# A list scheduler's figures at the second norm of a decoder layer: longer planned times, two loads counted as landed, the scaled epsilon on its own

## The chip, the cores and the metric

The kernel runs on one core of a Trainium2 chip. The metric is the device time of one execution in microseconds (us), lower is better. TensorE (PE in the profile) multiplies, VectorE (DVE) and ScalarE (ACT) do elementwise work, SyncE (SP) and GpSimd (POOL) issue most of the transfers.

## The reference

One layer of a hybrid decoder trunk on 256 tokens and 16 learned meta tokens, width 2048, all in fp32. Two token mixers and their gates give `h`, and the part that matters here follows:

```python
h = h + rms_norm(m @ w_o[l], g_post_mix[l])
u = rms_norm(h, g_pre_mlp[l])                       # the second norm
f = jnp.square(jax.nn.relu(u @ w_up[l])) @ w_down[l]   # 2048 -> 8192 -> 2048
h = h + rms_norm(f, g_post_mlp[l])                  # the third norm
```

## The kernel before

Every fp32 weight is loaded in chunks of 1 MB and split in two fp32r parts that TensorE can multiply: ScalarE casts the high part (`hi`), VectorE subtracts it from the raw chunk (`lo`). The MLP runs in pieces of 1024 hidden columns. A product of the up projection (U...) uses a chunk of 1024 rows by 256 columns, 128 of the columns for each of two banks. Names of products: `U1a0` is an up product of half 1, pair a, first half of the rows of w_up; `U1a1` the second half; both write the banks u0 and u1, as `U1b0` and `U1b1` do after them. `X...` are down products into the banks x00 to x11, `P...` and `Q...` are products of a Strassen-like scheme.

Around the second norm the order is: the last up products of pair 0 (`last_of_first`, into x00 to x11, called acc_up in the profile), then `FIRST_PIECE = "U1a0 U1a1 U1b0 R U1b1"` (L1388), then X3. The up products start on `h` that is not normed yet: the norm's factor of each token is applied later. For this, eight squares (`square_h1`, ScalarE, one for each token tile and block of 512 columns; L987 in the profile) add up the rows, `mean2` (VectorE, L1540 and L1541) and `root2` (ScalarE, L1545) give the root, and `diag2` (VectorE) makes the factor `r2` with a Newton step (L446 to L450), splits it in a power of two `p2` (L1550) and a mantissa, writes `p2` into a diagonal (L1553) and works out a scaled epsilon `eps2` from the mantissa (L1554 to L1558). The power of two goes through TensorE (`R`: `rows2`, L478) to `rb` (L1846); relu times `rb` (L1603) follows, and `u2` itself is multiplied by it (`scale_u2`, L1566). The mantissa is left out of the up and down products and comes back only as `eps2` in the third norm, at the end of the kernel (`norm3.start` in `before_last`).

After each pair of up products `up_pair` adds the two halves of the bank: ScalarE copies the one (L1578), VectorE adds the other (L1585). The next product into the same bank waits for that.

The order of the instructions on each engine in this part comes from a list scheduler that runs while the kernel is built (`Plan`, L23). Each item has an engine, a planned cost, and names that it reads and writes; `late` is added to the time until its result is there (a transfer's landing), and 0.15 (`HOP`) when the result goes to another engine. TensorE and SyncE keep the order in which their items were added. A due time is worked backwards: TensorE's items are due when the planned costs of the products ahead of them are used up, and all others so early that the items after them can be on time:

```python
due[i] = min(due[i], due[a] - cost - late - self.HOP)
...
first = min(begin(i) for i in can)
i = min((i for i in can if begin(i) <= first + self.HOP), key=lambda i: (due[i], i))
```

So on each engine, of the items that could begin within 0.15 of the earliest, the one due first is taken; an item with a late due time still takes a gap if nothing else can begin. The instructions are written out in the order of the planned starts, and each engine then works strictly in that order and waits by semaphores. The planned costs say nothing to the chip but this order.

The chunks of this part are loaded into five rooms (`raw_a`, `raw_c`, and three called `raw_m`) by `load` (L1449), in the order in which they are used: raw_a for U1b0, raw_c for U1b1, then X3 and so on; a room is loaded again when its chunk has been split (`split_raw`, L1487: cast on ScalarE at L1496, low part on VectorE at L1500). `kept` (L1830) stores `h` to memory for the end. The `bring` items (L1518) are loads by GpSimd's queue that add onto a chunk in its room.

Of the kernel before, what the change touches and what calls it, by code (L numbers as in the profile page):

```python
# [10 lines left out]
I32 = mybir.dt.int32  # L11
AF = mybir.ActivationFunctionType
ALU = mybir.AluOpType
# [102 lines left out]
def hybrid_block(ctx: ExitStack, tc: tile.TileContext, ins: dict, out: bass.AP):  # L116
    nc = tc.nc
# [34 lines left out]
    def f32(ap):  # L152
        return ap.bitcast(F32)
# [12 lines left out]
    late = []  # L166
# [34 lines left out]
    NB = D // CW  # L201
# [174 lines left out]
    ssq = const.tile([P, NT + 1, 2], F32, name="ssq")  # L376
# [67 lines left out]
    def rsqrt(r, q, var):  # L444

        nc.vector.reciprocal(r, q)  # L446
        nc.vector.tensor_mul(q, r, r)
        nc.vector.tensor_mul(q, q, var)
        nc.vector.tensor_scalar(q, q, -0.5, 1.5, op0=ALU.mult, op1=ALU.add)
        nc.vector.tensor_mul(r, r, q)  # L450
# [359 lines left out]
    def block(n):  # L810
        return slice(n * CW, (n + 1) * CW)
# [131 lines left out]
    h1 = big.tile([P, NT, D], F32, tag="k8", bufs=2, name="h1")  # L943
# [41 lines left out]
    def square_of(src, norm, t, n, scale=1.0):  # L985
        junk = tmp.tile([P, CW], F32, tag="junk", bufs=1, name=f"sq_{norm}_{n}_{t}")
        nc.scalar.activation(junk, src, AF.Square, scale=scale, accum_out=norm[:, t, n:n + 1])  # L987
# [14 lines left out]
    plan = Plan()  # L1002
# [20 lines left out]
    room_at = {(1, 0): 0, (2, 0): 1}  # L1023
# [176 lines left out]
    for i, s in enumerate(steps):  # L1200
# [5 lines left out]
        if s == "X30":  # L1206
            for t in range(NT):
                plan.add("PE", 0.0, lambda t=t: banks_o.update({f"c{t}3": acc_tile(f"o_c{t}3")}),
                         writes=(f"c{t}3", f"c{t}0"))
# [8 lines left out]
        if s == "X13":  # L1218
            for t in range(NT):
                plan.add("DVE", 0.4, lambda t=t: norm1.start(t), reads=(f"ssq{t}",),  # L1220
                         writes=(f"v{t}",))
# [142 lines left out]
    for b in range(2):  # L1364
        room = big.tile([P, b * LINE + KD * T], F32R, tag=f"s{b}", name=f"forms_{b}")
# [21 lines left out]
    plan = Plan()  # L1387
# [27 lines left out]
    def source(what, i):  # L1415
        if what[0] == "U":
            h, pr, c = int(what[1]), "ab".index(what[2]), int(what[3])
            return columns(w_up, c * HALF[0], HALF[0], i * PF + h * CW + pr * HALF_CW, HALF)[0]
        h, n = AT[what]
        return columns(w_down, (i * 2 + h) * KH, KH, n * CW)[0]  # L1420
# [26 lines left out]
    room_at = {}  # L1447

    def load(r):  # L1449
        src, (rows, width) = source(*r)  # L1450
        room = room_at[r] = free_rooms.pop(0)
        plan.add("SP", 3.1, lambda: nc.sync.dma_start(
            room_of[room].rearrange("p (k c) -> p k c", k=rows), src),
            writes=(f"raw{room}",), late=3.6)

    def loads():
        while to_load and free_rooms:
# [72 lines left out]
    ssq2 = const.tile([P, NT, NB], F32, name="ssq2")  # L1530
    r2, p2, eps2 = (const.tile([P, NT], F32, name=n) for n in ("r2", "p2", "eps2"))
    EXPONENT, MANTISSA, ONE = 0x7F800000, 0x007FFFFF, 0x3F800000
    box2 = {}

    def square_h1(t, n):
        return lambda: square_of(h1[:, t, block(n)], ssq2, t, n)
# [9 lines left out]

    def diag2():
        rsqrt(r2, box2["q"], box2["v"])
        bits, p_bits, e_bits = (x_.bitcast(I32) for x_ in (r2, p2, eps2))
        nc.vector.tensor_scalar(p_bits, bits, EXPONENT, None, op0=ALU.bitwise_and)  # L1550
        box2["diag"] = tmp.tile([P, T], F32R, tag="junk", bufs=1, name="diag2")
        for t in range(NT):
            nc.vector.tensor_scalar_mul(box2["diag"][:, t * P:(t + 1) * P], ident, p2[:, t:t + 1])  # L1553
        nc.vector.tensor_scalar(e_bits, bits, MANTISSA, ONE, op0=ALU.bitwise_and,  # L1554
                                op1=ALU.bitwise_or)
        for _ in range(2):
            nc.vector.tensor_mul(eps2, eps2, eps2)
        nc.vector.reciprocal(eps2, eps2)  # L1558
        nc.vector.tensor_scalar(eps2, eps2, RMS_EPS, None, op0=ALU.mult)
# [4 lines left out]
    def scale_u2(g):  # L1564
        both_ = u2[:, g * CK:(g + 1) * CK].rearrange("p k a t -> p (k a) t")
        plan.add("DVE", 2.22, lambda: nc.vector.tensor_mul(  # L1566
            both_, f32(both_), rb[:, None, :T].broadcast_to([P, 2 * CK, T])),
            reads=("rb",), writes=(f"u2{g // 2}",))
# [71 lines left out]
    def free_from(h, i):  # L1640

        return max(last_reader.get((h_, i), -1) for h_ in range(h + 1))

    def into_forms(h, pr, i, s_name, box):
        G, A, ks = forms[h], f"A{h}{pr}", slice(2 * pr, 2 * pr + 2)

        n = 2 if h or i == NP - 1 or "X1" in MODES[i] else 1

        def dst(part):
            return G[:, A1:A1 + n, ks, part, :]  # L1650

        def src():
            return box["s"].rearrange("p j (f t) -> p f j t", f=2)[:, :n]
        if i < NP - 1 and h == 1:
            def a_(f):
                return box["s"][:, :, f * P:(f + 1) * P]
            plan.add("DVE", 0.35, lambda: nc.vector.scalar_tensor_tensor(
                Q[:, S2Q, ks, :], Q[:, S3Q, ks, :], -1.0, a_(A2), op0=ALU.mult, op1=ALU.subtract),
                reads=(s_name, f"q3{pr}"), writes=(f"q3{pr}",))
            plan.add("DVE", 0.35, lambda: nc.vector.tensor_add(  # L1660
                Q[:, S4Q, ks, :], a_(A1), Q[:, S2Q, ks, :]),
                reads=(s_name, f"q3{pr}"), writes=(f"q4{pr}",))
        plan.add("ACT", 0.1 + 0.215 * n, lambda: nc.scalar.copy(dst(0), src()), reads=(s_name,),
                 writes=(A,))
        plan.add("DVE", 0.08 + 0.27 * n, lambda: nc.vector.tensor_sub(dst(1), src(), f32(dst(0))),
                 reads=(s_name, A), writes=(A + "l",))
        if i == NP - 1:
            return
        if h == 0 and pr == 1:
            split_form(0, S3, "S3", S3Q, "q3")  # L1670
        if h == 1 and pr == 1:
            split_form(0, S1, "S1", S1Q, "q1")
            split_form(1, S2, "S2", S2Q, "q3")
            split_form(1, S4, "S4", S4Q, "q4")
# [148 lines left out]
    for j in range(4):  # L1823
        plan.add("PE", 1.36, last_of_first(j), reads=(f"hi{q0}", f"lo{q0}"),
                 writes=(f"x{j // 2}{j % 2}",))
    loads()
    for t in range(NT):
        for n in range(NB):
            plan.add("ACT", 0.65, square_h1(t, n), reads=("h1",), writes=("junk", "ssq2"))
    kept = dram.tile([P, NT, D], F32, name="kept_h1")  # L1830
    plan.add("SP", 6.4, lambda: nc.sync.dma_start(kept, h1), writes=("h1", "hi3", "lo3"), late=4.0)
    plan.add("DVE", 0.4, mean2, reads=("ssq2",), writes=("v2",))
    plan.add("ACT", 0.3, root2, reads=("v2",), writes=("q2",))
    plan.add("DVE", 1.2, diag2, reads=("q2", "v2"), writes=("diag2",))
    for pr in range(2):
        up_done(0, pr, 0, accs[2 * pr:2 * pr + 2], [f"x{pr}{j}" for j in range(2)])

# [2 lines left out]
    for at_step[0], (s, i) in enumerate(steps):  # L1840
        for rest in [rest for rest in deferred if at_step[0] > free_from(rest[0], rest[2] - 1)]:
            deferred.remove(rest)
            into_forms(*rest)
        if s == "R":
            plan.add("PE", 0.9, rows2, reads=("diag2",), writes=("b",))
            plan.add("DVE", 0.4, lambda: nc.vector.tensor_copy(rb[:, :T], banks["b"][:, :T]),  # L1846
                     reads=("b",), writes=("rb",))
            for rest in unscaled:
                relu_squared(*rest)
            continue  # L1850
        if s[:3] == "add":
            continue
        for w in range(m_, min(m_ + 4, len(products))):
            if before.get(w, -1) >= m_:
                break
            weights(w)
        if m_ >= tail:
            break
        {"U": product_up, "X": product_plain, "P": product_block, "Y": product_last,
         "Q": product_block}[s[0]](m_, s, i)  # L1860
        m_ += 1
        if (s, i) == ("U1b1", 0):
            for g in range(KD // CK):
                scale_u2(g)

# [4 lines left out]
             writes=(f"raw{room_g}",), late=2.0)  # L1872
    for t in range(NT):
        plan.add("SP", 3.1, lambda t=t: nc.sync.dma_start(room_of[rooms_h[t]][:, :D], kept[:, t]),
                 reads=("h1",), writes=(f"raw{rooms_h[t]}",), late=2.0)
# [10 lines left out]
    def sum_of_squares(t, n):  # L1886
        src, name = tokens_of(t, n)
        plan.add("ACT", 0.65, lambda: square_of(src, norm3.ssq, t, n), reads=(name,),
                 writes=("junk", f"ssq{t}{n}"))

    def times_g(t, n):
        src, name = tokens_of(t, n)
        plan.add("DVE", 0.62, lambda: nc.vector.tensor_mul(
            dst_of(t, n * CW, (n + 1) * CW), src, g_mlp[:, block(n)]),
            reads=(name, f"raw{room_g}"), writes=(f"out{t}{n}", name if n < 2 else f"raw{room_f}"))

    def before_last(t):

        sum_of_squares(t, NB - 2)
        times_g(t, NB - 2)  # L1900
        plan.add("DVE", 0.4, lambda: norm3.start(t, eps2[:, t:t + 1]),
                 reads=[f"ssq{t}{n}" for n in range(NB - 1)], writes=(f"v{t}",))

    for t in range(NT):
        for n in range(NB - 2):
# [37 lines left out]
    for e, cs in enumerate(col_halves):  # L1943
        for w, s in ends:
# [3 lines left out]
                reads=half_names(w) + act_names(h, A2), writes=("ab"[e],))  # L1948

        def half_done(e=e, cs=cs):  # L1950
# [6 lines left out]
            if e == 0:  # L1957
# [12 lines left out]
                 writes=("junk", "v1", f"raw{room_f}", "out13") + (("r1",) if e else ()))  # L1970
# [28 lines left out]
```

## Time and profile before

| what | value |
|---|---|
| timed runs | median 1194.74 us (1194.17, 1194.74, 1195.89) |
| profiled execution, its own time | 1199.05 us |
| its span, first to last instruction | 1197.3 us |
| mean granted TensorE clock | 0.996 |
| PE, DVE, ACT busy | 1180.4, 1020.5, 680.9 us |
| all waits of TensorE that the view of waits lists | 8.5 us |

The table is read from the top down: the timed runs are what counts, the profiled execution is where durations come from. It took 1.75 us more than its span, and 4.31 us more than the timed median. In the rows of the timeline the columns are start, duration, engine, line, operation, result<-operands, shapes and count, and in square brackets the idle time of the engine ahead of the row and what ended it. Rows with a count above 1 are merged.

### The profile page before, as it was taken

What the parts mean: (1) busy time and instruction counts of PE and PEld (TensorE: products, weight loads), DVE (VectorE), ACT (ScalarE), POOL (GpSimd) and SP (SyncE); (2) the same over time, 40 slices, a digit from 0 to 9 for tenths busy, and PEclk for the clock granted to TensorE, in tenths of its full rate; (3) what the DMA queues carried; (4) which work ended last, traced back from release to release, by engine and by line L of the source; (5) the groups of instructions that cost most, each with busy time, mean ns of one, the idle gap of its engine ahead of it and who ended that gap; (6) DMA issues with size and microseconds to landing.
All of it is one profiled execution on the core that took longest, in us unless ns stands there. A gap on an engine that the chain in (4) does not pass through costs nothing.

```text
span 1197.3 us, 15759 instructions
## 1 busy us (share of the span) xinstructions
PE 1180.4 (99%) x6363; PEld 1023.7 (85%) x6363; DVE 1020.5 (85%) x1097; ACT 680.9 (57%) x705; POOL 41.8 (3%) x48
## 2 busy tenths in 40 slices
PE   9999999999999999999999999999999999999997
PEld 9999988888888888897888888888888888887886
DVE  6899978999776778677988989899999889898965
ACT  6533344444583455565666657666666676676742
POOL 1000000000000000000000000000000000000000
PEclk9999999999999999999999999999999999999999
DMA  9655555656548578548779889898998988998971
GB/s 291 212 177 179 185 197 179 207 179 205 182 165 282 172 251 264 198 135 290 211 210 260 242 243 273 248 262 230 274 249 253 259 265 243 250 262 232 271 255 71
DMA packets 176811, 269.76 MB, mean 225 GB/s; under 512 B 4610, under 2 KB 92866, under 8 KB 175841
## 3 DMA queue, kind: packets, MB, share of 16 engines
q1 hardware_dynamic: 160432, 234.83, 59.1%
q0 software_dynamic: 15408, 32.66, 14.9%
q10 hardware_dynamic: 896, 1.25, 0.3%
q8 instruction: 50, 0.82, 0.3%
q14 instruction: 25, 0.20, 0.0%
HBM read 264.53 MB, written 4.19 MB: 224 GB/s over the span
## 4 chain that ended last, share of the span: by engine, by line
PE 87%; DMA 6%; DVE 2%; ACT 2%; issue 2%; DVEq 0%; POOLq 0%; ACTq 0%; SPq 0%
PE acc_gate L789 15%; PE bank_u L496 14%; PE bank_a L1715 9%; PE bank_u L502 7%; PE acc_up L1715 7%; PE o_c L1128 6%; DMA raw_m<-in_w_down_dram 6%; PE bank_b L1715 5%; PE acc_z L491 4%; PE acc_co L789 4%; PE acc_po L789 4%; PE acc_v L491 3%; PE acc_g L491 3%; PE acc_vg L491 2%; PE bank_u L1715 1%
## 5 line engine op out<-in xcount | busy, mean ns | idle before, releaser
L496 PE MATMUL bank_u<-m,hi 128*128 128x512 f32 x960 | 331.1, 391 | 2.6 <-DVE F_raw L1585 2.6
L502 PE MATMUL bank_u<-m,lo 128*128 128x256 f32 x960 | 265.9, 277 | 0.0
L276 ACT CAST hi<-raw 128x2048 fp32r<-128x2048 f32 (+2 forms) x94 | 151.0, 1619 | 191.5 <-PE acc_gate L789 64.0
L1500 DVE TENSOR_TENSOR lo<-raw_m,hi 128x2048 fp32r<-128x2048 f32 x85 | 194.4, 2287 | 34.2 <-ACT hi L1496 34.2
L496 PEld LDWEIGHTS bank_u<-m,hi 128*128 128x128 f32 x960 | 180.9, 188 | 41.1 <-DVE F_raw L1585 3.0
L279 DVE TENSOR_TENSOR lo<-raw,hi 128x2048 fp32r<-128x2048 f32 (+2 forms) x94 | 180.1, 1924 | 37.1 <-ACT hi L276 36.4
L1496 ACT CAST hi<-raw_m 128x2048 fp32r<-128x2048 f32 x85 | 161.8, 1911 | 75.1 <-PE bank_a L1715 23.0
L502 PEld LDWEIGHTS bank_u<-m,lo 128*128 128x128 f32 x960 | 180.9, 188 | 1.6
L789 PE MATMUL acc_gate<-hi,u_um 128*128 128x512 f32 x416 | 131.1, 389 | 0.0
L557 DVE SCALAR_TENSOR_TENSOR c<-a,taps,c 128x256 f32<-128x256 f32 x240 | 115.6, 483 | 6.8
L789 PEld LDWEIGHTS acc_gate<-hi,u_um 128*128 128x128 f32 x416 | 78.1, 188 | 16.1
L789 PE MATMUL acc_gate<-lo,u_um 128*128 128x512 f32 x208 | 80.9, 389 | 0.0
L1715 PE MATMUL bank_a<-hi,forms 128*128 128x512 f32 (+1 forms) x232 | 75.7, 388 | 4.1 <-DVE F_raw L1744 4.1
L1715 PE MATMUL bank_b<-hi,forms 128*128 128x512 f32 (+1 forms) x208 | 67.4, 386 | 0.0
L1128 PE MATMUL o_c<-hi,m 128*128 128x512 f32 x208 | 65.6, 390 | 0.0
L1578 ACT COPY half<-bank_u 128x256 f32<-128x256 f32 x60 | 22.3, 372 | 73.6 <-PE bank_u L502 73.6
L1715 PE MATMUL bank_a<-fourth_pair,forms 128*128 128x512 f32 (+1 forms) x252 | 59.9, 386 | 0.7 <-ACT st_Q L1753 0.7
L1500 DVE TENSOR_TENSOR lo<-raw_a,hi 128x2048 fp32r<-128x2048 f32 x21 | 48.0, 2286 | 12.4 <-ACT hi L1496 12.4
L1715 PEld LDWEIGHTS bank_a<-hi,forms 128*128 128x128 f32 x232 | 43.4, 188 | 15.1 <-issue 5.2
L1500 DVE TENSOR_TENSOR lo<-raw_c,hi 128x2048 fp32r<-128x2048 f32 x20 | 45.7, 2287 | 10.9 <-ACT hi L1496 10.9
L1715 PEld LDWEIGHTS bank_a<-fourth_pair,forms 128*128 128x128 f32 x252 | 45.2, 188 | 10.1 <-ACT st_Q L1753 1.1
L1496 ACT CAST hi<-raw_a 128x2048 fp32r<-128x2048 f32 x21 | 40.1, 1910 | 20.6 <-PE bank_u L496 10.8
(398 smaller groups left out, 2267.2 us busy)
## 6 DMA issues: line engine op xcount, KB each, us to landing
raw<-in_w_in_dram SPq DMA_DIRECT2D x52, 1024.0 KB, 5.1
raw_m<-in_w_up_dram SPq DMA_DIRECT2D x42, 1024.0 KB, 7.2
raw_m<-in_w_down_dram SPq DMA_DIRECT2D x35, 1024.0 KB, 5.3
raw_a<-in_w_down_dram SPq DMA_DIRECT2D x15, 1024.0 KB, 5.7
raw_c<-in_w_down_dram SPq DMA_DIRECT2D x14, 1024.0 KB, 5.8
raw_m<-in_w_down_dram POOLq DMA_DIRECT2D x12, 1024.0 KB, 10.8
raw_o<-in_w_o_dram SPq DMA_DIRECT2D x10, 1024.0 KB, 7.2
raw_a<-in_w_up_dram SPq DMA_DIRECT2D x9, 1024.0 KB, 7.5
```

Of the source, the lines that this page charges most:

```text
L276: nc.scalar.copy(hi[:, sl, cs], raw[:, sl, cs])
L279: nc.vector.tensor_sub(lo[:, sl, cs], raw[:, sl, cs], f32(hi[:, sl, cs]))
L491: nc.tensor.matmul(acc, w[:, k[0], cs], act[:, k[1], a, off:], start=first and n == 0, stop=last and n == 2)
L496: nc.tensor.matmul(acc.rearrange("p (a t) -> p a t", a=2)[:, :, ts], hi[:, k[0], cs], act[:, k[1], :, off + ts.start:off + ts.stop], start ...
L502: nc.tensor.matmul(acc[:, :T], lo[:, k[0], cs], act[:, k[1], 0, off:], start=False, stop=stop, skip_group_check=True)
L557: nc.vector.scalar_tensor_tensor(c, conv["a"][:, q, i:i + T], taps[:, q, i:i + 1], c, op0=ALU.mult, op1=ALU.add)
L789: nc.tensor.matmul(acc, act(kk)[:, a_, ts_], w_[:, k, :], start=kk == 0 and n == 0, stop=kk == nk - 1 and n == 2)
L1128: nc.tensor.matmul(acc, form(k, a_), box[w_][:, k, :], start=start and k == 0 and n == 0, stop=stop and k == CK - 1 and n == 2, skip_group ...
L1496: nc.scalar.copy(box["hi"], raw)
L1500: nc.vector.tensor_sub(box["lo"], raw, f32(box["hi"]))
L1578: nc.scalar.copy(box[j], accs[j][:, :T])
L1715: nc.tensor.matmul(acc, forms[h][:, f, k, a_, :], box[w_][:, k, cs], start=start and k == 0 and n == 0, stop=stop and k == KH - 1 and n == ...
```

## The change

The first two loads of the last plan are planned with no cost on SyncE's queue and a landing after 1 and 2 instead of 3.1 and 3.6. The squares are planned at 0.75 instead of 0.65, `diag2` at 1.7 instead of 1.2. The five instructions of the scaled epsilon leave `diag2` and become an item of VectorE of their own (`eps_of_scaled`), planned at 0.9; it is added to the list behind U1b1 of the second piece, and `norm3.start` now names `eps2` as what it reads, so that its due time comes from there.

```diff
@@ -1449,9 +1449,10 @@
     def load(r):
         src, (rows, width) = source(*r)
         room = room_at[r] = free_rooms.pop(0)
-        plan.add("SP", 3.1, lambda: nc.sync.dma_start(
+        ahead = len(room_at) <= 2
+        plan.add("SP", 0.0 if ahead else 3.1, lambda: nc.sync.dma_start(
             room_of[room].rearrange("p (k c) -> p k c", k=rows), src),
-            writes=(f"raw{room}",), late=3.6)
+            writes=(f"raw{room}",), late=len(room_at) if ahead else 3.6)
@@ -1546,13 +1547,15 @@
     def diag2():
         rsqrt(r2, box2["q"], box2["v"])
-        bits, p_bits, e_bits = (x_.bitcast(I32) for x_ in (r2, p2, eps2))
+        bits, p_bits = (x_.bitcast(I32) for x_ in (r2, p2))
         nc.vector.tensor_scalar(p_bits, bits, EXPONENT, None, op0=ALU.bitwise_and)
         box2["diag"] = tmp.tile([P, T], F32R, tag="junk", bufs=1, name="diag2")
         for t in range(NT):
             nc.vector.tensor_scalar_mul(box2["diag"][:, t * P:(t + 1) * P], ident, p2[:, t:t + 1])
-        nc.vector.tensor_scalar(e_bits, bits, MANTISSA, ONE, op0=ALU.bitwise_and,
-                                op1=ALU.bitwise_or)
+
+    def eps_of_scaled():
+        nc.vector.tensor_scalar(eps2.bitcast(I32), r2.bitcast(I32), MANTISSA, ONE,
+                                op0=ALU.bitwise_and, op1=ALU.bitwise_or)
         for _ in range(2):
             nc.vector.tensor_mul(eps2, eps2, eps2)
         nc.vector.reciprocal(eps2, eps2)
@@ -1826,12 +1829,12 @@
-            plan.add("ACT", 0.65, square_h1(t, n), reads=("h1",), writes=("junk", "ssq2"))
+            plan.add("ACT", 0.75, square_h1(t, n), reads=("h1",), writes=("junk", "ssq2"))
...
-    plan.add("DVE", 1.2, diag2, reads=("q2", "v2"), writes=("diag2",))
+    plan.add("DVE", 1.7, diag2, reads=("q2", "v2"), writes=("diag2",))
@@ -1862,6 +1865,8 @@
             for g in range(KD // CK):
                 scale_u2(g)
+        if (s, i) == ("U1b1", 1):
+            plan.add("DVE", 0.9, eps_of_scaled, reads=("diag2",), writes=("eps2",))
@@ -1899,7 +1904,7 @@
         plan.add("DVE", 0.4, lambda: norm3.start(t, eps2[:, t:t + 1]),
-                 reads=[f"ssq{t}{n}" for n in range(NB - 1)], writes=(f"v{t}",))
+                 reads=["eps2"] + [f"ssq{t}{n}" for n in range(NB - 1)], writes=(f"v{t}",))
```

## The prediction

> **What bounds the kernel now.** I read the page first, for who is busy; then the waits of TensorE; then the stretch around its longest wait, engine by engine in order of time. Page of the profile:
>
> ```profile
> span 1197.3 us, 15759 instructions
> ## 1 busy us (share of the span) xinstructions
> PE 1180.4 (99%) x6363; PEld 1023.7 (85%) x6363; DVE 1020.5 (85%) x1097; ACT 680.9 (57%) x705; POOL 41.8 (3%) x48
> ```
>
> TensorE is busy for 1180.4 of 1197.3 us. A scheduler that leaves the products alone can win only what TensorE waits, and what it runs slowly because it waited. Two lines of the view of waits, TensorE's own (total, times, longest):
>
> ```profile
> PE bank_a L1715 <- DVE F_raw L1744: 4.1, 3, 1.7
> PE bank_u L496 <- DVE F_raw L1585: 2.6, 1, 2.6
> ```
>
> The second line is the longest single wait, and it is in the stage that the diff touches: U1b0 cannot write bank u0 before VectorE has added up the two halves of U1a (L1585). Windows around it, and one behind another wait, for the granted clock (PEclk):
>
> ```profile
> core 0: us, PE busy (x) PEld busy (x) DVE busy (x) ACT busy (x) POOL busy (x), PEclk, DMA share, GB/s
> 542.00:547.60 5.60, 5.60 (x34) 4.70 (x32) 4.38 (x15) 3.11 (x4) 0.00 (x0) 1.00 1.11 415
> 547.60:550.25 2.65, 0.00 (x2) 0.00 (x1) 2.65 (x4) 2.17 (x2) 0.00 (x0) 0.97 0.94 362
> 550.25:553.56 3.31, 3.31 (x10) 2.83 (x11) 2.47 (x2) 0.00 (x0) 0.00 (x0) 0.51 1.04 352
> 553.56:557.45 3.89, 3.89 (x25) 3.38 (x24) 0.00 (x0) 0.00 (x0) 0.00 (x0) 1.00 1.06 375
> 1089.24:1092.55 3.31, 3.31 (x15) 2.75 (x16) 3.31 (x2) 3.28 (x3) 0.00 (x0) 1.00 0.60 187
> ```
>
> TensorE does nothing for 2.65 us, and then runs at a granted clock of 0.51 for 3.31 us: ten matmuls, which at the rate of the first row (5.60 / 34 = 0.165 us) take 1.65. So the wait costs 2.65 + 1.66 = 4.3 us. Why was VectorE late? Its timeline:
>
> ```profile
> 540.81 0.16 DVE L1540 TENSOR_REDUCE tot<-ssq 128x2 f32<-128x8 f32 x1 [0.95 <-ACT ng_offset=None)_3_1_4612 L987]
> 541.01 0.17 DVE L1541 TENSOR_SCALAR tot<-tot 128x2 f32<-128x2 f32 x1
> 541.08 0.41 DVE L1585 TENSOR_TENSOR F_raw<-half,acc_up 128x256 f32<-128x256 f32 x1
> 542.88 2.29 DVE L1500 TENSOR_TENSOR lo<-raw_a,hi 128x2048 fp32r<-128x2048 f32 x1 [1.38 <-ACT hi L1496]
> 545.08 0.16 DVE L446 RECIPROCAL r<-rs_q 128x2 f32<-128x2 f32 x1
> ...
> 546.67 0.16 DVE L1554 TENSOR_SCALAR eps<-r 128x2 int32<-128x2 int32 x1
> ...
> 547.57 2.29 DVE L1500 TENSOR_TENSOR lo<-raw_c,hi 128x2048 fp32r<-128x2048 f32 x1
> 549.78 0.74 DVE L1585 TENSOR_TENSOR F_raw<-half,bank_u 128x256 f32<-128x256 f32 x2
> 550.44 2.28 DVE L1500 TENSOR_TENSOR lo<-raw_m,hi 128x2048 fp32r<-128x2048 f32 x1
> 557.76 0.42 DVE L1846 COPY rb<-bank_b 128x256 f32<-128x256 f32 x1 [5.04 <-PE bank_b L478]
> ...
> 561.69 1.28 DVE L1665 TENSOR_TENSOR forms<-F_raw,forms 128x512 fp32r<-128x512 f32 x2
> ```
>
> Ahead of the sums of U1a (549.78) stand, without a pause, the low part of raw_a, diag2 (545.08 to 546.67), the scaled epsilon (546.67 to 547.57) and the low part of raw_c. The first of them waited for ScalarE's cast of raw_a. ScalarE's timeline:
>
> ```profile
> 532.59 1.91 ACT L276 CAST hi<-raw 128x2048 fp32r<-128x2048 f32 x1 [2.39 <-DMA raw<-in_w_up_dram]
> 534.40 0.62 ACT L987 ACTIVATE ng_offset=None)_0_0_4564<-h 128x512 f32<-128x512 f32 x1
> ...
> 540.06 0.63 ACT L987 ACTIVATE ng_offset=None)_3_1_4612<-h 128x512 f32<-128x512 f32 x1
> 540.59 0.19 ACT L987 ACTIVATION_READ_ACCUMULATOR ng_offset=None)_3_1_4612<-h 128x1 f32 x1
> 540.69 0.35 ACT L1578 COPY half<-acc_up 128x256 f32<-128x256 f32 x1
> 540.94 1.91 ACT L1496 CAST hi<-raw_a 128x2048 fp32r<-128x2048 f32 x1
> 542.74 0.20 ACT L1545 ACTIVATE rs_q<-tot 128x2 f32<-128x2 f32 x1
> 542.84 1.90 ACT L1496 CAST hi<-raw_c 128x2048 fp32r<-128x2048 f32 x1
> 544.92 0.37 ACT L1578 COPY half<-bank_u 128x256 f32<-128x256 f32 x1 [0.18 <-PE bank_u L502]
> 547.64 0.37 ACT L1578 COPY half<-bank_u 128x256 f32<-128x256 f32 x1 [2.35 <-PE bank_u L502]
> ```
>
> All eight squares and four half copies come ahead of the cast of raw_a, and they start at 534.40, because the cast before them waited for a load.
>
> **The change part by part.** No multiplication, transfer or byte is added; the cost of the diff is an order. I work the order out by hand from the scheduler's rules (costs and due times are the ones in the code; they say who goes first, and I take no time from them). Zero is the first product of last_of_first; TensorE's planned costs put U1a0 at 5.44 (4 x 1.36), U1a1 at 10.88, U1b0 at 16.32 and R at 21.76 (2 x 2.72 each).
>
> Loads. Planned before, raw_a landed at 3.1 + 3.6 + 0.15 = 6.85, behind all squares (8 x 0.65 + 4 x 0.28 = 6.32). Now it has landed at 1.15, and its cast can begin as soon as last_of_first has let go of its buffer: 5.44 + 0.15 = 5.59. Its low part is due 2.22 + 0.15 before 16.32, the cast itself 1.83 + 0.15 before that: 11.97.
>
> Squares and diag2. With 1.7, diag2 is due at 21.76 - 1.85 = 19.91, the root at 19.46, the mean at 18.91, the last square (0.75) at 18.01, each earlier square 0.9 sooner. ScalarE's plan: three squares, a half copy, three squares, two half copies, the seventh square from 5.34 to 6.09. Then the cast (due 11.97) wins over the last half copy (due 17.18) and the last square (18.01). The mean, which needs that square, now comes on VectorE behind the low part of raw_a (planned 8.07 to 10.29) and the last acc_up sum, to 11.04. The cast of raw_c may begin at 11.03, the root only at 11.19, so the cast goes first and the root ends at 13.16. On VectorE the low part of raw_c may begin at 13.01, diag2 at 13.31: the former goes first, to 15.23. Then the sum of bank u0 (due 16.32 - 0.5 = 15.82) wins over diag2 (19.91). New VectorE order: low raw_a, last acc_up sum, mean, low raw_c, **sum of u0**, diag2, sum of u1, epsilon, low raw_m. The epsilon has a due time near the kernel's end and takes the first gap, 17.63 to 18.53, before the low part of raw_m can begin at 18.73. From there each item is held by a product or its operands, not by a load, so the plan returns to the old order.
>
> Now the measured durations in that order. One square with its half copy, 540.06 to 540.94, is 0.88 us, and these two leave the front of raw_a's cast: 540.06 instead of 540.94. Both loads are there:
>
> ```profile
> 526.16 0.51 SPq L1452 DMA_DIRECT2D raw_a<-in_w_up_dram  x1
> 526.77 2.52 SPq L1452 DMA_DIRECT2D raw_c<-in_w_up_dram  x1
> raw_a<-in_w_up_dram SPq DMA_DIRECT2D x2, 1024.0 KB, 10.0
> ...
> raw_c<-in_w_up_dram SPq DMA_DIRECT2D x1, 1024.0 KB, 12.4
> ```
>
> raw_a lands at 536.2, raw_c at 539.2. Low raw_a then starts at 542.88 - 0.88 = 542.00. Starts on VectorE are 2.20 apart behind a low part (542.88 to 545.08), so the last sum is at 544.20 and, 0.33 later (half of what the pair at 549.78 took to 550.44), the mean at 544.53; the mean takes 0.27 (540.81 to 541.08): low raw_c at 544.80. Its cast: raw_a's 1.80, half copy 0.25, square 0.63 after 540.06, so 542.74 to 544.65, in time. The sum of u0 starts at 547.00 and ends at 547.42; TensorE may write u0 about 0.05 later (550.20 to 550.25 in the old run), at 547.47. It needs the bank at 547.60. The wait is gone, with 0.13 us to spare; I charge 0.1 for errors of that size, since all these terms come from single rows. Gain 4.3 - 0.1 = **4.2 us**, if the clock stays full.
>
> What is late next? Diag2 now runs from 547.33 and takes 1.59: to 548.92, and R wants it 5.44 us behind 547.6. The sum of u1 stands behind diag2 and is done at 549.4; U1b0 needs u1 at 547.60 + 2.72 = 550.32. The epsilon's 0.90 us (five instructions) hide at 549.3 to 550.2 and push low raw_m to 550.2, 0.2 earlier than now; with no cover they would cost 0.9. SyncE's queue keeps its order; it waits for low raw_a and low raw_c, 0.9 and 2.8 us earlier, so the reloads of both rooms go out sooner. Behind R the steps hang on R itself: rb waited 5.04 us for it, the forms end at 562.97, 5.21 after rb began, and X3 began at 563.21 (5.45 after it):
>
> ```profile
> 563.21 0.39 PE L1715 MATMUL acc_up<-hi,forms 128*128 128x512 f32 x1
> 1089.24 0.47 PE L1715 MATMUL bank_a<-hi,forms 128*128 128x512 f32 x1 [1.67 <-DVE F_raw L1744]
> ```
>
> That margin of 0.24 us is the next thing to run out; U1b1 at the rate before the wait takes 0.2 us less, which just uses it up. I take nothing for it; between a gain of 0.2 and a loss of 0.2.
>
> Clock. The row of 550.25 says that 2.65 us of idle cost 1.66 more; the wait of 1.67 us ahead of 1089.24 left the clock at 1.00. The Trainium skill, TensorE: Matmul & The Clock Gate, section "Part 1: The HAM clock gate (the "warmup" mystery)", has the clock halved after an idle window of about 3.4 us, counted in free-running windows, so that it varies from run to run. Read literally a wait of 2.65 us does not fill a window; the trace shows the halved clock all the same. By the page the gain could be the wait alone, 2.6; by the row it is 4.2.
>
> The sum stands against the profiled execution, 1199.05 us (1197.3 and 1.75 around it). The timed median is 1194.74, 4.31 less: something in it is shorter without the profiler, and this wait may be part of that. Taking the profile's gain whole: 1194.74 - 4.15 = **1190.6 us**.
>
> **The rivals.** A measurement of this kernel can tell about 0.2%, 2.4 us, from no change.
>
> Only the wait. If in the timed runs the wait falls so that the clock is never halved, 2.65 - 0.1 is won: 1192.2 us. For it: at 1.67 us no halving, so a bound lies somewhere between; the three timed runs spread over 1.72 us, the size of one such event. Against it: the one profiled case has it. This is also where the page's free-running window would lead.
>
> The wait is shorter without the profiler. ScalarE's start at 534.40 hangs on a load that it waited 2.39 us for. If that lands 1 us sooner, everything up to 549.78 is 1 us sooner: the wait is 1.65, too short to halve the clock, and 1.6 are won: 1193.1 us. If 2.4 sooner, the gain is 0.2: 1194.5.
>
> The order does not turn out. The low part of raw_c wins over diag2 by 0.15 in the plan. If diag2 keeps its place, its 1.59 stand ahead of the sum: a wait of about 1.5, clock full; the gain is 4.3 - 1.5 = 2.8: 1191.9 us.
>
> Slower. Behind 800 us three waits for L1744 (4.1 us together) come from accumulating loads:
>
> ```profile
> raw_m<-in_w_down_dram POOLq DMA_DIRECT2D x12, 1024.0 KB, 10.8
> ```
>
> If TensorE, 4 us further on, meets them so that each of the three waits grows from 1.37 to 2.65 and halves the clock, they cost 3 x (1.28 + 1.66) = 8.8, less 4.2: 1199.3 us. It decides from about 2.65 us a wait. Against it: these loads are issued when VectorE frees a room, so they move along with the products.
>
> **How the numbers follow.** Forecast 0.54, only the wait 0.14, shorter wait 0.16, other order 0.06, slower 0.10. The forecast's own range is 1189.0 (0.2 for U1b1, and one of the three late waits of 1.37 gone by chance) to 1191.9. The range reaches up to 1193.6, over "only the wait", "other order" and more than half of the shorter wait, and leaves out slower (0.10), the rest of the shorter wait (0.06) and 0.04 below. Faster by over 0.2% (under 1192.35): 0.54, 0.08 of the second case and 0.05 of the fourth, 0.67. Slower 0.10; the rest, 0.23, is within 0.2%.
>
> **What would show it.** Right: no wait of bank_u for L1585 in TensorE's list, a granted clock of 1.00 from 547 to 553, the cast of raw_a ahead of the last square, the sum of u0 directly behind low raw_c and ahead of L446, the five epsilon instructions behind the sum of u1, X3 starting near 559. Wrong: a wait above 0.5 us at U1b0, diag2 still ahead of low raw_c, a new wait at X3 for L1665, or the waits for L1744 grown beyond 4.1 us.

## The result, and the profile after

The changed kernel takes 1192.68 us (median of 22 runs, 1190.43 to 1194.93), the kernel before in the same series 1194.73 us (22 runs, 1192.45 to 1197.66). The ratio is 0.998, 95% interval 0.9972 to 0.9988: about 2 us faster, with 1.4 to 3.3 us inside the interval. The forecast was 4.15 us. The profiled execution of the changed kernel took 1192.99 us, its span 1191.2 us.

The view of TensorE's waits, changed kernel (total, times, longest; its lines stand up to three further down than before):

```profile
PE bank_a L1718 <- DVE F_raw L1747: 2.6, 2, 1.5
PE idle L392 <- DVE rb L308: 1.1, 1, 1.1
PE bank_a L1718 <- ACT st_Q L1756: 0.7, 1, 0.7
```

The wait of bank_u for the sums of U1a is gone from it. The windows of the same stretch say that TensorE is busy all through, at the full granted clock (PEclk, the third number from the end):

```profile
547.60:550.25 2.65, 2.65 (x17) 2.31 (x16) 1.96 (x10) 2.17 (x2) 0.00 (x0) 1.00 0.95 371
550.25:553.56 3.31, 3.31 (x20) 2.89 (x19) 2.04 (x2) 0.21 (x1) 0.00 (x0) 1.00 1.04 379
```

ScalarE's timeline, changed kernel:

```profile
531.71 1.91 ACT L276 CAST hi<-raw 128x2048 fp32r<-128x2048 f32 x1 [1.75 <-DMA raw<-in_w_up_dram]
533.52 0.62 ACT L987 ACTIVATE ng_offset=None)_0_0_4566<-h 128x512 f32<-128x512 f32 x1
...
539.18 1.90 ACT L1497 CAST hi<-raw_a 128x2048 fp32r<-128x2048 f32 x1
540.97 0.38 ACT L1581 COPY half<-acc_up 128x256 f32<-128x256 f32 x1
541.24 0.65 ACT L987 ACTIVATE ng_offset=None)_3_1_4653<-h 128x512 f32<-128x512 f32 x1
541.77 0.20 ACT L987 ACTIVATION_READ_ACCUMULATOR ng_offset=None)_3_1_4653<-h 128x1 f32 x1
542.00 1.91 ACT L1497 CAST hi<-raw_c 128x2048 fp32r<-128x2048 f32 x1
544.04 0.20 ACT L1546 ACTIVATE rs_q<-tot 128x2 f32<-128x2 f32 x1
```

The cast of raw_a stands ahead of the last half copy and the last square, and the cast of raw_c ahead of the root. VectorE's timeline:

```profile
541.11 2.29 DVE L1501 TENSOR_TENSOR lo<-raw_a,hi 128x2048 fp32r<-128x2048 f32 x1 [1.93 <-ACT hi L1497]
543.32 0.42 DVE L1588 TENSOR_TENSOR F_raw<-half,acc_up 128x256 f32<-128x256 f32 x1
543.65 0.15 DVE L1541 TENSOR_REDUCE tot<-ssq 128x2 f32<-128x8 f32 x1
543.84 0.17 DVE L1542 TENSOR_SCALAR tot<-tot 128x2 f32<-128x2 f32 x1
543.95 2.29 DVE L1501 TENSOR_TENSOR lo<-raw_c,hi 128x2048 fp32r<-128x2048 f32 x1
546.16 0.41 DVE L1588 TENSOR_TENSOR F_raw<-half,bank_u 128x256 f32<-128x256 f32 x1
546.49 0.16 DVE L446 RECIPROCAL r<-rs_q 128x2 f32<-128x2 f32 x1
...
548.17 0.42 DVE L1588 TENSOR_TENSOR F_raw<-half,bank_u 128x256 f32<-128x256 f32 x1
548.51 0.16 DVE L1557 TENSOR_SCALAR eps<-r 128x2 int32<-128x2 int32 x1
...
549.98 2.29 DVE L1501 TENSOR_TENSOR lo<-raw_m,hi 128x2048 fp32r<-128x2048 f32 x1 [0.51 <-ACT hi L1497]
```

This is the order that the prediction works out, place by place: sum of u0 behind low raw_c, then diag2, sum of u1, epsilon, low raw_m. The sum of u0 ends at 546.57, and U1b0 starts at 547.57 by itself, so 1.0 us are to spare, not 0.13. The difference is where ScalarE starts: 533.52 here, 534.40 in the first profile of the kernel before. From that start to the end of the sum of u0 the prediction has 547.42 - 534.40 = 13.02 us, the chip 546.57 - 533.52 = 13.05.

```profile
553.23 0.28 PE L478 MATMUL bank_b<-diag,ones 128*128 128x256 f32 x1
558.78 0.40 PE L1718 MATMUL acc_up<-hi,forms 128*128 128x512 f32 x1
```

In TensorE's timeline R starts at 553.23 and X3 at 558.78, the latter 4.43 us ahead of the first profile of before, close to the forecast. So between these two profiles the whole gain is there, and another 1.5 us in the later waits for L1744 (4.1 us before, 2.6 here), which the change does not aim at. Between the timed runs the gain is half of the forecast. That is the question of the experiments.

### The profile page after: what moved, and what is told of

It reads as the page before. It is cut to its first block, busy times and chain, and to the rows that moved or that the text cites. A ratio compares the mean times of both kernels' runs of the same rounds, so it can differ in the third digit from the quotient of the medians.

```text
span 1191.2 us, 15760 instructions
## 1 busy us (share of the span) xinstructions
PE 1178.4 (99%) x6363; PEld 1022.6 (86%) x6363; DVE 1020.9 (86%) x1097; ACT 681.4 (57%) x705; POOL 41.8 (4%) x48
## 4 chain that ended last, share of the span: by engine, by line
PE 92%; DMA 4%; DVE 1%; issue 1%; ACT 1%; SPq 0%; DVEq 0%; POOLq 0%; ACTq 0%
PE bank_u L496 16%; PE acc_gate L789 15%; PE bank_a L1718 10%; PE bank_u L502 8%; PE acc_up L1718 7%; PE o_c L1128 6%; PE bank_b L1718 6%; PE acc_z L491 4%; DMA raw_m<-in_w_down_dram 4%; PE acc_co L789 4%; PE acc_po L789 4%; PE acc_v L491 3%; PE acc_g L491 3%; PE acc_vg L491 2%; PE acc_up L496 1%
## 5 line engine op out<-in xcount | busy, mean ns | idle before, releaser
L1497 ACT CAST hi<-raw_a 128x2048 fp32r<-128x2048 f32 x21 | 40.1, 1909 | 19.6 <-PE bank_u L496 10.8
```

Of the source, the lines that this page charges most:

```text
L1497: nc.scalar.copy(box["hi"], raw)
```

## The experiments

Theory A: the first profile of the kernel before is typical (wait 2.65 us, clock halved behind it), and part of the 4.2 us is given back later. Theory B: the wait is typical, the halved clock is not. Theory C: the wait itself is mostly shorter, because ScalarE's load lands sooner than in that profile. The times are medians with their number of runs; ratios are against the kernel before, in runs beside it, with a 95% interval.

**E1, the kernel before again.** No edit.

> The kernel before, once more and against itself: how long is the wait at U1b0, and is the clock halved behind it, in an execution other than the one of the first profile? Theory A (profile typical, gain given back later): wait of bank_u 2.4 to 2.7 us, clock near 0.5 behind it for about 3.3 us, span like the first. Theory B (the wait, but not the halved clock): wait 2.4 to 2.7 us, clock 1.00. Theory C (a shorter wait in most executions, because the load that ScalarE starts behind lands sooner): wait 0.5 to 1.7 us, clock 1.00. Ratio 1.000 within its interval in all.

Median 1196.22 us (11) against 1195.48 (35): ratio 1.0009 (0.9997 to 1.0022). That is the same kernel twice, so a difference of about 1 us between two series of this size means nothing by itself. From its profile, ScalarE's timeline, then TensorE's, then a window behind the wait:

```profile
531.55 1.91 ACT L276 CAST hi<-raw 128x2048 fp32r<-128x2048 f32 x1 [1.56 <-DMA raw<-in_w_up_dram]
```

```profile
549.21 0.50 PE L496 MATMUL bank_u<-m,hi 128*128 128x512 f32 x1 [1.53 <-DVE F_raw L1585]
554.96 0.28 PE L478 MATMUL bank_b<-diag,ones 128*128 128x256 f32 x1
560.73 0.39 PE L1715 MATMUL acc_up<-hi,forms 128*128 128x512 f32 x1
```

```profile
549.25:552.50 3.25, 3.25 (x19) 2.84 (x20) 2.53 (x2) 0.64 (x1) 0.00 (x0) 1.00 1.00 347
```

The load landed 1.04 us sooner than in the first profile (by the start of its cast), the wait is 1.53 instead of 2.65, the clock behind it is full, and from the start of U1b0 to R TensorE takes 554.96 - 549.21 = 5.75 us, against 3.31 + 3.89 = 7.20 in the first profile. X3 starts at 560.73: the changed kernel's 558.78 is 1.95 us ahead of this, not 4.43. That is theory C.

**E2, E3: extra matmuls.** At the start of U1b0, eleven matmuls in the kernel before (E2), twelve in the changed one (E3):

```diff
+        if (s, i) == ("U1b0", 0):
+            def filler():
+                off = u2.shape[3] - T
+                for _ in range(11):            # E3: 12, E5: 6, E6: 36
+                    nc.tensor.matmul(banks["a"].rearrange("p (a t) -> p a t", a=2), ones,
+                                     u2[:, 0, :, off:off + T], start=True, stop=True,
+                                     skip_group_check=True)
+            plan.add("PE", 0.0, filler)
```

> The kernel before with eleven extra matmuls of 0.227 us (2.5 us, into the idle bank a) between U1a1 and U1b0, so that TensorE is busy through the wait and the halved clock has no cause. Theory A: 1.6 us faster than before. Theory B: the same time within 0.5 us. Theory C: slower, by what the filler is longer than the wait, 1 to 2 us.

> The changed kernel with twelve extra matmuls of 0.227 us (2.7 us) at the same place: TensorE reaches R and X3 2.7 us later than in the changed kernel, without any idle time. If everything behind is paced by TensorE, it takes 2.7 us more than the changed kernel (1192.7 + 2.7 = 1195.4, 0.6 above before). If a lead is given back later (theory A), it takes under 1 us more than the changed kernel (below 1193.7).

E2: 1193.70 us (12), ratio 0.9987 (0.9976 to 0.9997): faster than before, by 0.4 to 2.9 us. This speaks for theory A, and against C, which has it slower. E3: 1195.25 us (12), ratio 0.9998 (0.9988 to 1.0008). As all the comparisons with before: the changed kernel at -3.3 to -1.4 us, E3 at -1.4 to +1.0; so 2.7 us of extra matmuls cost between nothing and 4 us, and E3 alone decides nothing. Both profiles have less of the later waits for `give` (VectorE adds a finished bank a to F; L1744 before, L1747 after) than the two kernels without the filler: 2.1 and 1.9 us against 3.0 (E1) and 2.6 (changed).

**E5, E6: less and more of it.** Six matmuls in the kernel before, 36 in the changed one.

> The kernel before with six extra matmuls (1.4 us) at the start of U1b0. They fit into the wait of 1.5 us of the second look as into the 2.65 us of the first, so they cost nothing by themselves, and what is left of the idle time (0.1 to 1.3 us) is too short to halve the clock. So the time that it gains is the halved clock alone. Theory A (clock halved in most executions): 1.6 us faster than before. Theory C (shorter wait, full clock in most): the same, within 0.5 us. A mixture lies between: gain / 1.66 is the share of executions with the halved clock.

> The changed kernel with 36 extra matmuls (8.2 us) instead of twelve. If all behind is paced by TensorE: 8.2 us above the changed kernel, 1200.9, 5.4 above a before of 1195.5, and 5.4 us above the run with twelve. If the later waits for L1744 give a part back, they vanish here and no more is given back than they cost: 8.2 less at most 3 us, 2.4 to 5.4 above before.

E5: 1195.38 us (12), ratio 1.000 (0.9987 to 1.0013). Taking the idle time away down to 0.5 us brought nothing that can be told from zero, which speaks against a halved clock in most runs; but the interval reaches from -1.6 to +1.6 us, so E5 alone does not settle it. E6: 1200.34 us (6), ratio 1.0047 (1.0033 to 1.0062), 5.6 us above before, where TensorE's pace alone has 5.4. From twelve to 36 matmuls (5.4 us more) the ratios rise by 0.0049, 5.9 us. So what TensorE loses here it gets back little of, if any (E6's interval is 4.0 to 7.4 us above before): theory A's give-back is not seen. The filled profiles have 1.8 (E6) to 2.1 us of later waits, those of the same orders without a long filler 2.4 to 4.2: why the long fillers lower them by about a us was not tried. Counting that us, E2's filler (2.7 us in place of a wait of 1.5 to 2.0) should end near the time of before, not 1.6 us below it: E2 stays in part unexplained.

**E4, E7, E8: the parts.** E4 has the loads and the longer times and leaves the epsilon in diag2. E7 has the loads alone, E8 the times alone (squares 0.75, diag2 1.7).

```diff
# E4 and E7
-        plan.add("SP", 3.1, ..., late=3.6)
+        ahead = len(room_at) <= 2
+        plan.add("SP", 0.0 if ahead else 3.1, ..., late=len(room_at) if ahead else 3.6)
# E4 and E8
-            plan.add("ACT", 0.65, square_h1(t, n), ...)
+            plan.add("ACT", 0.75, square_h1(t, n), ...)
-    plan.add("DVE", 1.2, diag2, ...)
+    plan.add("DVE", 1.7, diag2, ...)
```

> Loads and longer times changed, the epsilon left inside diag2: the order differs from the changed kernel in one place, the epsilon (0.9 us) ahead of the sum of bank u1. That sum would end at 550.3, where U1b0 needs it at 550.3: 0 to 0.2 us above the changed kernel, so all of the gain, 2.0 us below before, comes from these two parts in every theory; if the epsilon's own item matters, more than 0.5 us of it is lost.

> Only the two loads are planned as landed, times as before. The order then differs from before in one place: the last half copy goes behind the cast of raw_a (0.13 us), diag2 and the epsilon stay ahead of the low part of raw_c. Every theory: wait of bank_u still 1.4 to 2.6 us, the time of before within 0.5 us. If the loads alone brought the gain, it would be 2 us faster.

> Only the longer planned times, loads as before. Squares and half copies change places among themselves, all eight squares still come ahead of the cast of raw_a, diag2 and the epsilon ahead of the low part of raw_c. Every theory: wait of bank_u still 1.5 to 2.7 us, the time of before within 0.5 us. If the times alone brought the gain, it would be 2 us faster. The wait in this look and the one with the loads alone also says how it goes with the landing of the load ahead of the squares: 1 us later is 1 us more of wait, and the clock halves only where the wait is near 2.6 us.

E4: 1193.44 us (12), ratio 0.9982 (0.9969 to 0.9995), the changed kernel's. E7: 1195.41 (12), ratio 0.9999 (0.9987 to 1.0011); E8: 1195.07 (12), 0.9998 (0.9987 to 1.0008). TensorE still waits for the sums of U1a, in the view of waits of E7, then of E8:

```profile
PE bank_u L496 <- DVE F_raw L1586: 1.9, 1, 1.9
```

```profile
PE bank_u L496 <- DVE F_raw L1585: 1.7, 1, 1.7
```

Neither part alone moves diag2 behind low raw_c, and neither gains. The two together do both. The epsilon's own item changes one place in the order, behind the sum of u1 instead of ahead of it, and nothing that could be measured. (Built alone, with the old times and loads, it leaves the order of ScalarE's and VectorE's instructions as it was: the epsilon takes the gap right behind diag2. No run has it alone.)

**E9, E10: the load lands later.** An extra copy of 1 MB, behind ScalarE's load in SyncE's queue, in the kernel before (E9) and in the changed one (E10):

```diff
     hi, lo = fetch()
     flush()
+    extra = dram.tile([P, D], F32, name="extra")
+    nc.sync.dma_start(extra, w_down[:P, :])
```

> The kernel before with an extra copy of 1 MB from memory to memory, issued right behind the load that ScalarE's squares wait for, so that this load lands later. If the wait at U1b0 hangs on that landing (it took 6.1 to 6.9 us in ten looks): every us of later landing is a us of wait more, and from about 2.6 us of wait the clock is halved behind it. With a landing at about 8 us: wait 3 to 3.5 us, clock 0.5, 2 to 3.5 us slower than before. If the wait does not hang on the landing: wait still 1.5 to 2 us, the same time.

> The changed kernel with the same extra copy. Its sum of u0 ended 1.1 us before TensorE wanted the bank, so of 1.5 to 2 us of later landing 0.4 to 0.9 us are left as a wait, with the clock full: 0.5 to 1 us above the changed kernel, 1 to 1.5 us below before. The gain of the change against the kernel with the same copy is then 3.5 to 5 us, as in the prediction, instead of 2.

E9: 1198.91 us (11) against 1195.35, ratio 1.0029 (1.0017 to 1.0041). E10: 1194.77 us (12), 0.9991 (0.9981 to 1.0002). E9: ScalarE's timeline, and two windows (the wait, and from there to R). E10: ScalarE's and TensorE's timelines.

```profile
534.09 1.91 ACT L276 CAST hi<-raw 128x2048 fp32r<-128x2048 f32 x1 [4.22 <-DMA raw<-in_w_up_dram]
```

```profile
547.55:551.75 4.20, 0.00 (x1) 0.00 (x1) 4.00 (x11) 2.17 (x2) 0.00 (x0) 1.00 1.06 441
551.75:559.00 7.25, 7.25 (x32) 6.24 (x33) 2.48 (x2) 0.00 (x0) 0.00 (x0) 0.76 1.01 363
```

```profile
533.93 1.90 ACT L276 CAST hi<-raw 128x2048 fp32r<-128x2048 f32 x1 [4.00 <-DMA raw<-in_w_up_dram]
```

```profile
548.85 0.50 PE L496 MATMUL bank_u<-m,hi 128*128 128x512 f32 x1 [1.52 <-DVE F_raw L1590]
```

The load lands 2.54 us later than in E1, more than expected, and the wait is 2.67 us longer: 4.20. From U1b0 to R it takes 7.25 us at a mean granted clock of 0.76. The changed kernel had 1.0 us to spare; its load lands 2.2 us later than in its own profile, which leaves 1.2 us, and the wait is 1.52 (TensorE was also there 0.24 us sooner, at 547.33). So the wait hangs on this landing, and under the same copy the change is worth 1198.91 - 1194.77 = 4.1 us. Against before, E10 is 0.6 us faster by the medians, 1.1 by the ratio, not clear of zero, where 1 to 1.5 were expected.

E9's profile, at 1202.76 us, is the slowest of its 11 runs, so it is no typical one either. It has a second halved clock, behind a later wait, the one for `give` (L1746 here):

```profile
1091.20 0.47 PE L1717 MATMUL bank_a<-hi,forms 128*128 128x512 f32 x1 [2.06 <-DVE F_raw L1746]
```

**E11, E12: without the later waits.** The accumulating loads (`bring`) planned to land after 6.0 instead of 4.0, in the changed kernel (E11) and in the kernel before (E12):

```diff
-                    reads=names, writes=names, late=4.0)
+                    reads=names, writes=names, late=6.0)
```

> The changed kernel with accumulating loads planned to land after 6.0 instead of 4.0 (they take 10.8 us, planned 5.5 + 4.0). VectorE then adds bank a to F ahead of the low parts and raw sums that wait for such loads, at places where TensorE waits for it (2.6 us in the look at the changed kernel). If these waits are what spreads the times: 1 to 2.5 us below the changed kernel, 3 to 4.5 below before. If other items come too late instead: the same or up to 3 us slower.

> The kernel before with the accumulating loads planned at 6.0 as in the last run, loads, squares, diag2 and epsilon as before: its order differs from that of the last run in the places of the change alone. With the later waits gone, what is left between the two is the wait at U1b0: if it is typically 1.5 to 2 us with a slow restart, and the clock halved in about one execution of seven, 2 to 2.5 us above the last run (1193.2 to 1193.7), with a wider spread than it has; if the first profile were typical, 4.2 us above it (1195.4); if the change worked by way of the later waits, the same as the last run (1191.2).

E11: 1191.21 us (5, from 1190.49 to 1191.69), ratio 0.9964 (0.9951 to 0.9977): faster than both kernels, by 4.1 us than before. E12: 1193.16 us (12, from 1192.91 to 1195.19), ratio 0.9987 (0.9977 to 0.9996). TensorE's waits, E11 first, then the first line of E12:

```profile
PE idle L392 <- DVE rb L308: 1.1, 1, 1.1
PE bank_a L1718 <- ACT st_Q L1756: 0.7, 1, 0.7
```

```profile
PE bank_u L496 <- DVE F_raw L1585: 2.0, 1, 2.0
```

E11 has no wait for `give` left. Between E11 and E12 the orders of VectorE and ScalarE differ only around the second norm, so what lies between them is the price of the wait at U1b0, measured with little else that varies: 1.95 us by the medians. The two ran in different series; by their ratios to the kernel before it is 2.7 us. With the later waits gone the times also lie closer: 1.2 us from lowest to highest in E11, 4.5 in the changed kernel. In E12's profile the wait is 2.0 us long, with the clock full behind it:

```profile
549.62:552.93 3.31, 3.31 (x19) 2.89 (x20) 2.55 (x2) 0.23 (x1) 0.00 (x0) 1.00 1.03 366
```

Ten of E12's twelve runs lie from 1192.91 to 1193.85, at mean granted clocks of 0.997 and 0.998. The two others took 1195.11 and 1195.19, both at 0.996, lower by about as much as 3.4 us at half clock take from the mean (1.7 / 1192 = 0.0014). That these two ran at the halved clock at U1b0 is read from the mean alone; no other wait in E12's profile is above 1.1 us.

## Why the prediction was right or wrong

The range held the time, and the direction was right; the central value was 2.1 us too low. The forecast's own part of the range, 1189.0 to 1191.9, did not hold 1192.68: the whole range did, because it was drawn over the rivals. "Faster by over 0.2%", at 0.67, did not come either: 1192.68 against 1194.73 is 0.17%.

- *Order, cover and what comes next*: right. The new order came out as worked by hand, the epsilon hid in its gap, and no new wait came at R or X3. Low raw_m ended 1.0 us ahead of R, and X3 began 5.55 us behind R, without a wait.
- *VectorE's chain from ScalarE's start to the sum of u0*: 13.02 us predicted, 13.05 measured.
- *The wait, 2.65 us*: mis-sized. Five other profiles in which the place is as before (E1, E7, E8, E12, and E5 with six matmuls in it) have 1.5 to 2.0 us; E5's 1.4 of filler and 0.5 of wait come to 1.9. The landing that it hangs on took 6.9 us in the first profile and 6.1 to 6.5 in these.
- *The clock, 1.66 us*: right in mechanism, a little too large, and wrong as a term of every run. From U1b0 to R the first profile took 7.20 us and E1 5.75, so the halved clock cost 1.45. At 1.5 to 2.0 us of wait at U1b0 the profiles have the full clock, at 2.65 and 4.20 the halved one. Of 103 timed runs of the kernel before that stood beside E1 to E12, 13 have a mean granted clock of 0.996, with a median of 1198.5 us; the other 90, from 0.997 up, one of 1195.0. The first profile, at 1199.05 us and 0.996, is like the 13. Of 69 timed runs without this wait (the changed kernel, E2, E3, E4, E6, E11) none is at 0.996, so the low mean goes with the wait. It is a rough sign: it does not say where the clock was halved, as E9's second case shows, and in every profile the clock is also at half for the last 3 to 6 us of the span, by a different length each time, so that a run at 0.997 can hold a halved stretch too.
- *Carrying the profile's gain to the median*: this is the step that failed. The prediction saw 4.31 us between the two, wrote that this wait may be part of it, and took the gain whole all the same. The rival "the wait is shorter without the profiler" has the right mechanism and, at 1193.1 us, nearly the time; but the profiler is not the reason. Profiled executions of the same kernel have the short wait as well: it is the landing that differs from one execution to the next. With 1.5 to 2.0 us of wait, and 1.45 us in at least 13 of 103 runs (0.2 on average), the gain would be 1.7 to 2.2 us, an estimate; 2.05 was measured.
- *The rule of the Trainium skill* (an idle window of about 3.4 us, free-running; TensorE: Matmul & The Clock Gate, section "Part 1: The HAM clock gate (the "warmup" mystery)"): an idle stretch under the window's length can halve the clock here (2.65 us, and 2.06 in E9), so a literal reading is too mild. That it varies from run to run agrees with E12, where two of twelve runs show the lower mean clock.
- *Slower, by the later waits*: did not come. They were 2.6 us in the changed kernel's profile, 2.4 to 4.2 in those of the kernel before (E5's among them) and of its single parts.

## What to carry to other kernels

Before a wait in one profile is priced, ask what it hangs on: a wait behind a transfer's landing is a sample, and so is the clock behind it; where the profiled execution is far above the timed median, the largest wait may be what makes it so. In a list scheduler parts of a change that do nothing alone (E7, E8) can do all of it together (E4), because the order flips only where due times and starts cross. Where a planned time is below the measured one, as with the accumulating loads (into raw_m 10.8 us to land in the first profile, planned 5.5 + 4.0), a longer one can be worth nearly as much again (E11).

## What the runs showed of the hardware that I had not expected

A longer idle stretch did not make the halved clock last longer. Behind 2.65 us of idle TensorE the way from U1b0 to R took 7.20 us, behind 4.20 us (E9) 7.25 us at a mean granted clock of 0.76, and behind 1.53 us (E1), with the clock full, 5.75 us: about 1.5 us more, or nothing.

The traces show how this goes. Ahead of the kernel's end they have three halved stretches, one in the first profile and two in E9, each 3.41 us long, and those of E9 start 539.3 us apart, which is 158 times 3.413. All full stretches between two changes of the clock, 542.72 us and 638.29 us in the first profile for example, are whole multiples of it too (159 and 187 times). So here the clock changes only in steps of 3.41 us, which lie differently against the kernel in each execution. The windows, cut at these steps: first profile, E12 (most of its wait lies in the first row), and E9's second case.

```profile
546.66:550.07 3.41, 0.94 (x6) 0.59 (x4) 3.27 (x8) 2.17 (x2) 0.00 (x0) 1.00 0.95 380
550.07:553.48 3.41, 3.23 (x10) 2.75 (x11) 2.65 (x3) 0.00 (x0) 0.00 (x0) 0.50 1.05 356
```

```profile
547.81:551.22 3.41, 1.59 (x9) 1.42 (x10) 3.41 (x4) 2.04 (x2) 0.00 (x0) 1.00 0.97 362
551.22:554.63 3.41, 3.41 (x21) 2.95 (x20) 0.95 (x1) 0.00 (x0) 0.00 (x0) 1.00 1.05 364
```

```profile
1088.56:1091.97 3.41, 1.35 (x7) 0.84 (x5) 3.41 (x3) 1.42 (x1) 0.00 (x0) 1.00 0.65 228
1091.97:1095.38 3.41, 3.41 (x10) 2.63 (x9) 3.41 (x2) 2.28 (x2) 0.00 (x0) 0.50 0.41 121
```

TensorE is idle for 2.47, 1.82 and 2.06 us of the first row of each, and the second row is halved, full, halved. In all 14 traces, their ends included, every step with 2.05 us or more of idle is followed by a halved one, and none with 1.84 us (E7) or less. So a wait of under about 2 us leaves the clock full wherever it lies, a longer one halves it if enough of it falls into one step, and one busy step behind it brings the full clock back.

The landing of one 1 MB load went from 6.1 us (E1) to 8.8 us (E9) when another 1 MB was copied beside it, and between the executions without a copy it spread from 6.0 (E11) to 6.9 us. What makes that spread was not tried.
